# Two score components in separate PSUM tiles, a new engine order, and raw weight tiles with two buffers in a two-layer diffusion backbone

## The chip, the cores and the metric

The kernel runs on one core of a Trainium2 chip. The metric is the device time of one execution in microseconds; lower is better. The core has TensorE (PE; its weight loads are listed as PEld), VectorE (DVE), ScalarE (ACT), GpSimd (POOL) and SyncE (SP), each with its own queue of instructions that it takes in order. SP issues nearly all DMA transfers here, so a transfer whose data isn't ready holds up all that stand behind it in SP's queue.

## The reference, cut to what matters

Two layers over 1024 tokens of width 1024, with 256 context tokens. Layer 0 has a short gated convolution and differential attention with 4 heads side by side, layer 1 a Fourier mixing; a squared-ReLU MLP follows each. The change lies in layer 0, in the input projections and the attention:

```python
def diff_attend(q, k, v, lam):                     # c: two components of each head
    s = jnp.einsum('bqhcd,bkhcd->bhcqk', q, k).astype(jnp.float32) * (DIFF_QK_DIM ** -0.5)
    p = jax.nn.softmax(s, axis=-1)
    pd = (p[:, :, 0] - lam * p[:, :, 1]).astype(v.dtype)
    return jnp.einsum('bhqk,bkhd->bqhd', pd, v)

u = modulate(h, sh1, sc1)                          # sh, sc, g: silu(c) @ ada_w + ada_b
p = u @ w_in[j]                                    # conv (3 x 512), q, k, v columns
k_all = jnp.concatenate([k, kc], axis=1)           # 1024 latent + 256 context keys
o = diff_attention_blocks(q, k_all, v_all, lam)    # 128 queries at a time
y = jnp.concatenate([conv_mixer(...), sub_ln(o, ...)], axis=-1) @ w_out_mix[j]
```

## The kernel before, in words

All products are made of rounded parts: a tensor is split into a high part (`ScalarE` copy to fp32r) and a low part (the difference), and a product is three matmuls, lines 87 to 89 (`mm3`). Times in microseconds below are from the span's start.

**Projections.** Twenty weight tiles of 128x1024, eight for q and k and twelve for the convolution, are loaded by SP (`w_load`, line 218), split by ScalarE (line 97) and GpSimd (line 98) into `wh` and `wl` (`w_parts`), and used by TensorE (`proj`). The raw tile `wraw` has one buffer, `wh` and `wl` have two. `next_weights(i)` splits tile i+1 and then loads tile i+2. In the q/k part each of four passes (q and k, two pairs of heads) makes blocks of 512 tokens (b0, b1, and for k the 256 context tokens), which are rotated on VectorE, GpSimd and ScalarE (`rotate`) into the tiles `rp0` to `rp3`, two buffers each, and stored to DRAM (line 398). `store(0)` issues all waiting stores but the last entry, so each block's stores leave one block later.

Between them VectorE sums up the modulation vectors of the layer (`Ada`): one tick adds one 128x512 tile `wa` of `ada_w` (load line 152, addition lines 158 and 160); eight ticks make a unit, which `ada_end` finishes some ticks later with one matmul `ag` (line 174). Four units are gate rows: their bias row is loaded into a tile of the same ring (line 177), added (line 179), and one row is stored to DRAM at once (line 181). The ring has 6 tiles, and loads run 5 ahead. In this part the order of every queue, SP's too, is the order of the program. The second half of the units runs in the convolution part, with a new pool. After convolution tile 8 SP loads the q/k sets of the first head (`load_set`, lines 496 to 499, eight transfers each) and its values.

**Attention.** 32 query tiles (8 for each head) of 128 rows, two of them a pair. For component c of a tile: S makes the scores of 1280 keys (six matmuls, lines 615 to 619), M their negated maximum (VectorE, line 622), E the exponential and its sum (ScalarE, line 627). The one PSUM tile `scores`, 128 x 2 x 1280, holds both components for the whole stage; component 0 has columns 0 to 1279 with the context keys last, component 1 columns 1280 to 2559 with the context keys first. CB makes the factor lambda over the sums (VectorE), PD scales component 1 (GpSimd, line 636), PE adds it to component 0 (GpSimd, line 640, as two pieces because the keys are ordered differently). Then in five rounds for a pair: T transposes two key blocks of both tiles (TensorE, four operations, line 654, tile `pt`, two buffers), H rounds (ScalarE, line 660), L takes the rest (VectorE, line 665), P multiplies with the values (six matmuls into `po`). OC copies `po` out, SQ squares (GpSimd), SS sums over a head's width (TensorE), SC updates the norm (VectorE, two operations, lines 693 and 694).

The order of PE, DVE, ACT and POOL is written out by the table `PIPE`: the time of each step in pairs after the pair's start; all steps of all pairs are sorted by pair + offset and issued in that order. SP's order in this stage comes from a planner. FR, FS and FL finish the rows of a head (a product on GpSimd, a rounded copy on ScalarE, the rest on VectorE, each for four quarters of 256 columns), X times the split of the output weights. A q/k set is reloaded into the buffers of an older one (`load_set(n)`, three sets in turn). When the scores are done, their space becomes the accumulators `bky` of the output projection (`open_rows`), for which 28 groups of three matmuls (`prefill`) are spread over the remaining steps.

Of the kernel before, what the change touches and what calls it, by code (L numbers as in the profile page):

```python
# [12 lines left out]
F32 = mybir.dt.float32  # L13
F32R = mybir.dt.float32r
AF = mybir.ActivationFunctionType
ALU = mybir.AluOpType
# [4 lines left out]
P = 128  # L21
N = 1024
NC = 256
D = 1024
KT = 8
NK = N + NC
# [4 lines left out]
FS = 1.0 / math.sqrt(1024.0 * 128.0)  # L31
# [6 lines left out]
def body(tc, nc, I, O, dbg=None):  # L38
# [104 lines left out]
    modp = {}  # L143
    gates = {}

    def ada_unit(wp, psp, ptag, l, which, half, steps=False, wab=3, **kw):
        c0 = which * D + half * 512
        acc = []

        def load(k):  # L150
            wa = wp.tile([P, 512], F32, name="wa", tag="wa", bufs=wab)
            nc.sync.dma_start(out=wa, in_=I["ada_w"][l, k * P:(k + 1) * P, c0:c0 + 512])
            return wa

        def add(k, wa):
            if k == 0:
                acc.append(wp.tile([P, 512], F32, name="aacc", tag="aacc", bufs=2 if steps else 3))
                nc.vector.tensor_scalar(acc[0], wa, cs[:, k, 0:1], None, ALU.mult)
            else:
                nc.vector.scalar_tensor_tensor(out=acc[0], in0=wa, scalar=cs[:, k, 0:1], in1=acc[0],  # L160
                                               op0=ALU.mult, op1=ALU.add)

        finish = lambda: ada_end(wp, psp, ptag, l, which, half, acc[0], wab, **kw)
        if steps:
            return load, add, finish
        for k in range(KT):
            add(k, load(k))
        return finish

    def ada_end(wp, psp, ptag, l, which, half, acc, wab, gate=None, col=None, plus=False, spill=None):  # L170
        c0 = which * D + half * 512
        if True:
            ps = psp.tile([P, 512], F32, name="ag", tag=ptag)
            nc.tensor.matmul(ps, ones, acc, start=True, stop=True)
            if gate is not None or spill is not None:
                gb = wp.tile([P, 512], F32, name="wa", tag="wa", bufs=wab)
                nc.sync.dma_start(out=gb, in_=I["ada_b"][l, c0:c0 + 512].partition_broadcast(P))
                dst = gate[:, half * 512:half * 512 + 512] if spill is None else gb
                nc.vector.tensor_tensor(out=dst, in0=ps, in1=gb, op=ALU.add)
                if spill is not None:  # L180
                    nc.sync.dma_start(out=spill[:, half * 512:half * 512 + 512], in_=gb[0:1, :])
                return
            t = wp.tile([P, 4, P], F32, name="wa", tag="wa", bufs=wab)
            for j in range(4):
                nc.vector.tensor_tensor(out=t[:, j, :], in0=ps[:, j * P:(j + 1) * P], in1=ident, op=ALU.mult)
            d = col[:, half * 4:half * 4 + 4]
            nc.vector.tensor_reduce(out=d, in_=t, axis=AX.X, op=ALU.add)
            b = adab[:, l * 48 + which * 8 + half * 4:l * 48 + which * 8 + half * 4 + 4]
            nc.vector.tensor_tensor(out=d, in0=d, in1=b, op=ALU.add)
            if plus:  # L190
                nc.vector.tensor_scalar(d, d, 1.0, None, ALU.add)


    ps1 = popen("ps1", bufs=4, space=PSUM)
# [10 lines left out]
    gate = {}  # L205
# [8 lines left out]

    def w_load(i):
        if i < len(wsrc):
            wraws[i] = pW.tile([P, D], F32, name="wraw", tag="wraw", bufs=1)
            nc.sync.dma_start(out=wraws[i], in_=wsrc[i])

    def w_parts(i):  # L220
# [133 lines left out]
    ada0 += [(4, h, dict(col=col["sc2"], plus=True)) for h in range(2)]  # L354
    ada0 += [(3, h, dict(col=col["sh2"])) for h in range(2)]
    tile_waits = dict(reuse_waits="tile")


    class Ada:
        AHEAD = 5  # L360

        def __init__(self, p, units):
            self.units = [ada_unit(p, ps1, "tr", 0, w, h, steps=True, wab=self.AHEAD + 1, **kw) for w, h, kw in units]
            self.n, self.m, self.wa, self.ends = 0, 0, {}, []
            self.load(self.AHEAD)

# [23 lines left out]
    Qd = [dram.tile([4, 4, 32, N], F32, name=f"Qd{i}") for i in range(2)]  # L390
    Kd = [dram.tile([4, 4, 32, NK], F32, name=f"Kd{i}") for i in range(2)]
    Ad = [dram.tile([KT, P, N], F32, name=f"Ad{i}") for i in range(2)]
    stores = []

    def store(*keep):
        while len(stores) > len(keep):
            for o, i in stores.pop(0):
                nc.sync.dma_start(out=o, in_=i)

    def next_weights(i):  # L400
        if i:
            w_parts(i + 1)
        w_load(i + 2)

    def proj(i, bH, bL, n, tag="mm"):
        ps = ps1.tile([P, 512], F32, name="pj", tag=tag)
# [106 lines left out]
    with tc.manual_schedule(engines={mybir.EngineType.PE, mybir.EngineType.DVE, mybir.EngineType.Activation,  # L513
# [41 lines left out]
        for c in range(12):  # L555
            i = 8 + c
# [25 lines left out]
    pclose("pC", "pW", "pGs", "pU")  # L582
    psS = popen("psS", bufs=1, space=PSUM, **tile_waits)
    psT = popen("psT", bufs=1, space=PSUM, side="right", **tile_waits)
    scores = psS.tile([P, 2, NK], F32, name="s")
    pA = popen("pA", bufs=2, side="left", **tile_waits)
    pGate = popen("pGate", side="right", **tile_waits)
    for n in ("g1", "g2"):
# [11 lines left out]
    class Tile:  # L600
# [5 lines left out]
        def S(self, c):  # L606
            if not self.sc:
                self.mx = pA.tile([P, 2], F32, name="mx", tag="mx", bufs=4)
            H = hsets[self.h, c]
            q = H["q"][:, self.qt * P:self.qt * P + P]  # L610
            t = self.sc[c] = scores[:, c, :]
            x = NC * c
            for o in (0, 512):
                ps = t[:, x + o:x + o + 512]
                nc.tensor.matmul(ps, q, H["k0"][:, o:o + 512], start=True, stop=False)  # L615
                nc.tensor.matmul(ps, q, H["k1"][:, o:o + 512], start=False, stop=True)
            ps = t[:, 0:NC] if c else t[:, N:NK]
            nc.tensor.matmul(ps, q, H["k0"][:, N:NK], start=True, stop=False)
            nc.tensor.matmul(ps, q, H["kx"], start=False, stop=True)

# [15 lines left out]
            nc.gpsimd.tensor_scalar(self.e[1], self.e[1], self.a, 0.0, ALU.mult, ALU.add)  # L636

        def PE(self):
            for o, i in ((slice(0, N), slice(NC, NK)), (slice(N, NK), slice(0, NC))):
                nc.gpsimd.tensor_tensor(out=self.e[0][:, o], in0=self.e[0][:, o], in1=self.e[1][:, i], op=ALU.add)  # L640

    class Pair:
        def __init__(self, p):
# [3 lines left out]

        def T(self, kp):
            pd = [tiles[2 * self.p + j].e[0] for j in range(2)]
            pt = psT.tile([P, 2, 256], F32, name="pt", tag="pt", bufs=2)  # L650
            for i in range(2):
                for j in range(2):
                    kt = kp * 2 + i
                    nc.tensor.transpose(pt[:, i, j * P:(j + 1) * P], pd[j][:, kt * P:(kt + 1) * P], ident)
            self.pt[kp] = pt
# [71 lines left out]
    def finish_last(A7):  # L727
        H = heads[3]
        A7.extend(p3a.tile([P, N], F32R, name=f"A7{i}", tag=f"A7{i}", bufs=1) for i in range(2))
        for hf in range(2):  # L730
            bc = psT.tile([P, 512], F32, name="bc", tag="pt", bufs=2)
# [105 lines left out]
    for h in range(4):  # L837
        k = PIPE["SC",] + 4 * h + 3
        at(k + 0.001, lambda h=h: finish_stats(h))
        if h < 3:  # L840
            for m in range(4):
                base = k + 0.6 + (m if h < 2 else m // 2 * 0.8)
                fr = base + (PIPE["FR",] - base) % 1.0
                fs, fl = (fr + PIPE[o,] - PIPE["FR",] for o in ("FS", "FL"))
                for t, f in ((fr, finish_rows), (fs, finish_split), (fl, finish_low)):
# [600 lines left out]


PIPE = {
    ("FR",): -6.2830,
    ("FS",): -6.0349,  # L1450
    ("FL",): -5.9476,
    ("S", 1, 0): 0.0000,
    ("M", 1, 0): 0.1528,
    ("S", 0, 0): 0.2550,
    ("E", 1, 0): 0.3415,
    ("M", 0, 0): 0.4838,
    ("S", 1, 1): 0.5563,
    ("E", 0, 0): 0.6288,
    ("M", 1, 1): 0.6786,
    ("S", 0, 1): 0.7886,  # L1460
    ("CB", 0): 0.8122,
    ("E", 1, 1): 0.8236,
    ("PD", 0): 0.8690,
    ("M", 0, 1): 0.9188,
    ("PE", 0): 0.9878,
    ("E", 0, 1): 1.0638,
    ("CB", 1): 1.2865,
    ("PD", 1): 1.3432,
    ("PE", 1): 1.4620,
    ("T", 0): 1.9563,  # L1470
    ("H", 0): 2.0114,
    ("L", 0): 2.0917,
    ("T", 1): 2.1677,
    ("T", 2): 2.2114,
    ("H", 1): 2.2367,
    ("H", 2): 2.2891,
    ("L", 1): 2.3319,
    ("T", 3): 2.4044,
    ("L", 2): 2.4227,
    ("P", 0): 2.4480,  # L1480
    ("T", 4): 2.5127,
    ("H", 3): 2.5354,
    ("L", 3): 2.6175,
    ("P", 1): 2.6594,
    ("P", 2): 2.7240,
    ("H", 4): 2.7703,
    ("L", 4): 2.8576,
    ("P", 3): 2.8917,
    ("P", 4): 3.1031,
    ("OC",): 3.2052,  # L1490
    ("SQ",): 3.2585,
    ("SS",): 3.3581,
    ("SC",): 3.3930,
    ("X",): 4.4830,
}

PERM = np.concatenate([np.arange(512), [512], 1024 - np.arange(1, 512)])
# [109 lines left out]
```

## Time and profile before

| | us |
|---|---|
| median of 3 runs (lowest, highest) | 2466.03 (2465.24, 2471.18) |
| profiled execution, its own time | 2469.14 |
| its span, first to last instruction | 2467.3 |
| PE busy | 2232.9 (90%) |
| VectorE, GpSimd, ScalarE busy | 1263.8 (51%), 1031.7 (42%), 692.7 (28%) |
| mean granted clock of TensorE | 0.962 |
| projections; attention with TensorE's tail | 113 to 418; 418 to 757 |

A busy share is a mean over stages with different limits, so each stage has to be read for itself. A matmul's duration in a row is modelled, since matmuls overlap; the distance from one start to the next tells what one costs the engine. "[1.66 <-DVE mx L622]" says that the engine sat idle for 1.66 us before this instruction and that the maximum of line 622 on VectorE ended the wait. The granted clock is 1.0 at 2.4 GHz and 0.5 at 1.2 GHz.

### The profile page before, as it was taken

Reading aid. Unit: us, or ns where it says so; the run is one execution under the profiler, and the core shown is the slowest. Engines: PE = TensorE matmul, PEld = TensorE weight load, DVE = VectorE, ACT = ScalarE, POOL = GpSimd, SP = SyncE. Lnnn points to the kernel's source line nnn. Section 1 sums busy time; section 2 is a strip of 40 time slices with the busy share of each in tenths; the row PEclk is TensorE's granted clock in tenths of the full one; section 3 lists DMA queues with packets and bytes.
Section 4 is the critical chain, followed back from the end, with each engine's and each line's share of the span. In section 5 each row is a group of like instructions: output and inputs, shape, how many; then the busy total and the mean of one; then the engine's idle time right before and its main releaser. Section 6 shows DMA issues by size and latency. Waiting matters only on the chain.

```text
span 2467.3 us, 26198 instructions
## 1 busy us (share of the span) xinstructions
PE 2232.9 (90%) x9978; PEld 1795.7 (73%) x9978; DVE 1263.8 (51%) x1751; ACT 692.7 (28%) x1039; POOL 1031.7 (42%) x736
## 2 busy tenths in 40 slices
PE   7988597567779899999999999989899999999998
PEld 4776485456667687777788887767678888788886
DVE  7455362456654677567643433745653433434335
ACT  5211011345543521112112222443612212122122
POOL 3333131465653543323345834555733333334131
PEclk9998798799989999999999999999999999999999
DMA  7344438044323634334322323343511111111111
GB/s 280 128 155 140 155 128 212 31 98 119 83 69 111 209 112 155 105 113 141 101 68 82 127 92 107 113 156 120 180 51 52 52 35 60 43 52 52 45 50 68
DMA packets 121869, 261.98 MB, mean 106 GB/s; under 512 B 14642, under 2 KB 44594, under 8 KB 121488
## 3 DMA queue, kind: packets, MB, share of 16 engines
q1 hardware_dynamic: 120704, 254.69, 31.8%
q0 software_dynamic: 1040, 5.62, 0.7%
q8 instruction: 78, 1.28, 0.2%
q14 instruction: 47, 0.39, 0.0%
HBM read 213.06 MB, written 47.21 MB: 105 GB/s over the span
## 4 chain that ended last, share of the span: by engine, by line
PE 61%; DMA 11%; DVE 10%; POOL 7%; ACT 5%; issue 4%; SPq 1%; POOLq 0%; ACTq 0%; DVEq 0%
PE bky L87 9%; PE bky L88 9%; PE bky L89 9%; PE bkh L89 7%; PE bkh L88 7%; PE bkh L87 7%; DVE mx L622 3%; DMA wa<-in_ada_w 3%; ACT e L627 2%; DVE aacc L160 2%; DMA wa<-in_ada_b 2%; PE s L615 2%; DMA Kd<-rp 1%; PE pj L89 1%; PE pj L87 1%
## 5 line engine op out<-in xcount | busy, mean ns | idle before, releaser
L1016 DVE TENSOR_TENSOR acc<-bky,acc 128x512 f32<-128x512 f32 x448 | 304.3, 688 | 321.6 <-PE bky L89 320.5
L87 PE MATMUL bky<-wh,hh 128*128 128x512 f32 x1024 | 402.8, 395 | 16.8 <-DVE acc L1016 14.7
L88 PE MATMUL bky<-wl,hh 128*128 128x512 f32 x1024 | 402.4, 393 | 0.0
L89 PE MATMUL bky<-wh,hl 128*128 128x512 f32 x1024 | 401.3, 392 | 0.0
L1000 POOL TENSOR_TENSOR hl<-r,hh 128x512 fp32r<-128x512 f32 x128 | 178.9, 1401 | 407.2 <-DVE r L999 398.4
L963 ACT CAST wh<-wraw 128x1024 fp32r<-128x1024 f32 x128 | 131.4, 1049 | 674.2 <-PE bky L89 479.7
L964 POOL TENSOR_TENSOR wl<-wraw,wh 128x1024 fp32r<-128x1024 f32 x56 | 137.3, 2457 | 300.0 <-ACT wh L963 300.0
L999 DVE TENSOR_TENSOR r<-r 128x512 f32<-128x512 f32 x128 | 119.4, 939 | 243.8 <-ACT hh L998 240.1
L87 PEld LDWEIGHTS bky<-wh,hh 128*128 128x128 f32 x1024 | 192.7, 188 | 67.2 <-DVE acc L1016 21.2
L88 PEld LDWEIGHTS bky<-wl,hh 128*128 128x128 f32 x1024 | 192.8, 188 | 43.2 <-issue 0.7
L89 PEld LDWEIGHTS bky<-wh,hl 128*128 128x128 f32 x1024 | 192.8, 188 | 42.4
L88 PE MATMUL bkh<-UB,wh 128*128 128x512 f32 x512 | 200.9, 393 | 0.7 <-POOL UB L133 0.7
L87 PE MATMUL bkh<-UB,wh 128*128 128x512 f32 x512 | 200.7, 393 | 0.0
L89 PE MATMUL bkh<-UB,wl 128*128 128x512 f32 x512 | 200.6, 392 | 0.0
L962 POOL TENSOR_TENSOR wraw<-wraw,gateg 128x1024 f32<-128x1024 f32 x64 | 156.6, 2447 | 97.6 <-DMA wraw<-in_w 90.2
L87 PE MATMUL bkh<-UA,wh 128*128 128x512 f32 x448 | 177.9, 397 | 0.0
L88 PE MATMUL bkh<-UA,wh 128*128 128x512 f32 x448 | 176.3, 394 | 0.0
L89 PE MATMUL bkh<-UA,wl 128*128 128x512 f32 x448 | 175.7, 394 | 0.0
L87 PE MATMUL pj<-UH,wh 128*128 128x512 f32 x320 | 134.0, 419 | 41.2 <-ACT wh L97 41.2
L160 DVE SCALAR_TENSOR_TENSOR aacc<-wa,cs,aacc 128x512 f32<-128x512 f32 x140 | 141.9, 1014 | 37.3 <-DMA wa<-in_ada_w 34.9
L622 DVE TENSOR_REDUCE mx<-s 128x1 f32<-128x1280 f32 x64 | 95.5, 1492 | 125.5 <-ACT e L627 125.1
L964 DVE TENSOR_TENSOR wl<-wraw,wh 128x1024 fp32r<-128x1024 f32 x72 | 118.2, 1649 | 77.5 <-ACT wh L963 77.4
(386 smaller groups left out, 4250.8 us busy)
## 6 DMA issues: line engine op xcount, KB each, us to landing
wraw<-in_w SPq DMA_DIRECT2D x128, 512.0 KB
wa<-in_ada_w SPq DMA_DIRECT2D x160, 256.0 KB
xt<-in_ada_w SPq DMA_DIRECT2D x16, 512.0 KB
xt<-in_x SPq DMA_DIRECT2D x16, 512.0 KB
acc<-Hd SPq DMA_DIRECT2D x16, 512.0 KB
wraw<-in_w_cv SPq DMA_DIRECT2D x12, 512.0 KB
aa<-Ad SPq DMA_DIRECT2D x16, 384.0 KB
k<-Kd SPq DMA_DIRECT2D x16, 320.0 KB
```

Of the source, the lines that this page charges most:

```text
L87: nc.tensor.matmul(ps, aH, bH, start=start, stop=False)
L88: nc.tensor.matmul(ps, aH, bL, start=False, stop=False)
L89: nc.tensor.matmul(ps, aL, bH, start=False, stop=stop)
L160: nc.vector.scalar_tensor_tensor(out=acc[0], in0=wa, scalar=cs[:, k, 0:1], in1=acc[0], op0=ALU.mult, op1=ALU.add)
L615: nc.tensor.matmul(ps, q, H["k0"][:, o:o + 512], start=True, stop=False)
L622: nc.vector.tensor_reduce(out=self.mx[:, c:c + 1], in_=self.sc[c], axis=AX.X, op=ALU.max, negate=True)
L962: nc.gpsimd.tensor_tensor(out=w, in0=w, in1=g, op=ALU.mult)
L963: nc.scalar.copy(wh, w)
L964: eng.tensor_tensor(out=wl, in0=w, in1=raw(wh), op=ALU.subtract)
L999: nc.vector.tensor_tensor(out=r, in0=r, in1=r, op=ALU.mult)
L1000: pace[0] = nc.gpsimd.tensor_tensor(out=hl[:, c], in0=r, in1=raw(hh[:, c]), op=ALU.subtract)
L1016: pace[1] = nc.vector.tensor_tensor(out=a[:, c], in0=ps, in1=a[:, c], op=ALU.add)
```

## The change

Projections: `wraw` gets two buffers; `next_weights` loads tile i+2 before it splits tile i+1; the `Ada` ring has 8 tiles for loads 7 ahead, and the tiles of `ada_end` come from a ring of their own (`wf`, two); the store of a gate row is put on the list `stores` and issued with the next stores.

Attention: each component has its own PSUM tile of 1280 columns, with the context keys last in both, and a buffer of its own; GpSimd's addition is one operation of 1280 columns; `pt` has one buffer instead of two, also for the broadcast in `finish_last`; the times at which the quarters of a head's rows are finished follow one formula for heads 0 to 2 (line 842); and `PIPE` has new offsets, with a pair's last step at 2.99 instead of 3.39.

```diff
-    def ada_unit(wp, psp, ptag, l, which, half, steps=False, wab=3, **kw):
+    def ada_unit(wp, psp, ptag, l, which, half, steps=False, wab=3, stores=None, **kw):
...
-        finish = lambda: ada_end(wp, psp, ptag, l, which, half, acc[0], wab, **kw)
+        finish = lambda: ada_end(wp, psp, ptag, l, which, half, acc[0], *(("wf", 2) if steps else ("wa", wab)), stores, **kw)
...
-                gb = wp.tile([P, 512], F32, name="wa", tag="wa", bufs=wab)
+                gb = wp.tile([P, 512], F32, name="wa", tag=wtag, bufs=wab)
...
-                if spill is not None:
+                if stores is not None:
+                    stores.append([(spill[:, half * 512:half * 512 + 512], gb[0:1, :])])
+                elif spill is not None:
                     nc.sync.dma_start(out=spill[:, half * 512:half * 512 + 512], in_=gb[0:1, :])
...
-            wraws[i] = pW.tile([P, D], F32, name="wraw", tag="wraw", bufs=1)
+            wraws[i] = pW.tile([P, D], F32, name="wraw", tag="wraw")
...
-        AHEAD = 5
+        AHEAD = 7
...
     def next_weights(i):
+        w_load(i + 2)
         if i:
             w_parts(i + 1)
-        w_load(i + 2)
...
-    scores = psS.tile([P, 2, NK], F32, name="s")
...
-            t = self.sc[c] = scores[:, c, :]
-            x = NC * c
+            t = self.sc[c] = psS.tile([P, NK], F32, name=f"s{c}", tag=f"s{c}")
             for o in (0, 512):
-                ps = t[:, x + o:x + o + 512]
+                ps = t[:, o:o + 512]
...
-            ps = t[:, 0:NC] if c else t[:, N:NK]
+            ps = t[:, N:NK]
...
-            for o, i in ((slice(0, N), slice(NC, NK)), (slice(N, NK), slice(0, NC))):
-                nc.gpsimd.tensor_tensor(out=self.e[0][:, o], in0=self.e[0][:, o], in1=self.e[1][:, i], op=ALU.add)
+            nc.gpsimd.tensor_tensor(out=self.e[0], in0=self.e[0], in1=self.e[1], op=ALU.add)
...
-            pt = psT.tile([P, 2, 256], F32, name="pt", tag="pt", bufs=2)
+            pt = psT.tile([P, 2, 256], F32, name="pt", tag="pt", bufs=1)
...
-                base = k + 0.6 + (m if h < 2 else m // 2 * 0.8)
+                base = k + 0.6 + m // 2 * 0.8
```

The new order within one pair's time, by engine, where a prime marks a step of the next pair's rounds, is: PE: S(1) of tile 0, T2, P0, P1, T3, P2, S(0) of tile 0, T4, P3, S(1) of tile 1, T0', P4, S(0) of tile 1, T1', SS. DVE: FL, L2, CB1, M, L3, M, L4, M, L0', CB0, M, L1', SC. ACT: E, H2, FS, H3, X, E, H4, E, H0', E, OC, H1'. POOL: PE0, PD1, PE1, FR, X's low part, PD0, SQ.

## Rows read from the trace of the kernel before

**Rows 1.** Stretches: length; PE, PEld, DVE, ACT, POOL busy; clock, DMA, GB/s
```profile
113.00:418.00 305.00, 254.00 (x1074) 203.68 (x1073) 141.33 (x201) 39.02 (x54) 76.72 (x43) 0.90 0.50 157
308.00:398.00 90.00, 90.00 (x392) 73.16 (x390) 47.84 (x77) 13.59 (x18) 24.46 (x12) 1.00 0.57 160
...
457.00:720.00 263.00, 181.88 (x1092) 156.88 (x1092) 162.06 (x225) 133.42 (x218) 166.15 (x121) 0.93 0.33 81
720.00:757.00 37.00, 35.34 (x198) 31.04 (x198) 8.84 (x19) 7.99 (x16) 8.04 (x9) 0.91 0.31 89
```

**Rows 2.** Waits of SP's queue, 113 to 418: total us, times, longest
```profile
SPq L218 <- POOL wl L98: 52.3, 11, 9.4
SPq L181 <- DVE wa L179: 37.0, 4, 10.5
```

**Rows 3.** TensorE in time order, behind idle stretches: start, us, [idle <-releaser]
```profile
183.61 0.80 PE L87 MATMUL pj<-UH,wh 128*128 128x512 f32 x1 [8.03 <-ACT wh L97]
186.10 0.80 PE L89 MATMUL pj<-UH,wl 128*128 128x512 f32 x1 [1.27 <-POOL wl L98]
...
291.57 0.79 PE L87 MATMUL pj<-UH,wh 128*128 128x512 f32 x1 [17.44 <-ACT wh L97]
...
403.95 0.80 PE L87 MATMUL pj<-UH,wh 128*128 128x512 f32 x1 [5.75 <-ACT wh L97]
```

**Rows 4.** SP in order of time: bias row, gate-row store, weight loads
```profile
262.67 3.26 SPq L177 DMA_DIRECT2D wa<-in_ada_b  x1
276.53 0.26 SPq L181 DMA_DIRECT2D G2d<-wa  x1
...
282.16 0.40 SPq L218 DMA_DIRECT2D wraw<-in_w_cv  x1
...
394.71 0.36 SPq L218 DMA_DIRECT2D wraw<-in_w_cv  x1
```

**Rows 5.** Waits of the engines, 418 to 757: total us, times, longest
```profile
DVE mx L622 <- ACT e L627: 125.1, 62, 8.3
```

**Rows 6.** Attention in order of time, one turn of maximum, scores, exponential
```profile
584.58 1.49 DVE L622 TENSOR_REDUCE mx<-s 128x1 f32<-128x1280 f32 x1 [2.37 <-ACT e L627]
...
586.12 0.50 PE L615 MATMUL s<-k,q 128*128 128x512 f32 x1 [1.66 <-DVE mx L622]
...
587.39 0.28 PE L87 MATMUL po<-ph,vs 128*128 128x256 f32 x1
...
587.64 1.33 ACT L627 ACTIVATE e<-s,mx 128x1280 f32<-128x1280 f32 x1 [2.62 <-PE s L619]
...
588.09 0.60 PE L654 MATMUL pt<-ident,e 128*128 128x128 f32 x4
...
589.09 1.49 DVE L622 TENSOR_REDUCE mx<-s 128x1 f32<-128x1280 f32 x1 [2.05 <-ACT e L627]
```

**Rows 7.** Groups by shape, 418 to 757: count, busy us, mean ns, idle before
```profile
L640 POOL TENSOR_TENSOR e<-e,e 128x1024 f32<-128x1024 f32 x32 | 75.6, 2363 | 2.1
L665 DVE TENSOR_TENSOR pl<-pt,ph 128x512 fp32r<-128x512 f32 x80 | 54.5, 682 | 19.2 <-ACT ph L660 19.1
...
L660 ACT CAST ph<-pt 128x512 fp32r<-128x512 f32 x80 | 45.7, 586 | 21.7 <-PE po L89 15.5 <-PE pt L654 6.0
...
L640 POOL TENSOR_TENSOR e<-e,e 128x256 f32<-128x256 f32 x32 | 23.8, 743 | 0.0
```

**Rows 8.** Attention in order of time, the two steps of SC and GpSimd beside them
```profile
577.58 1.34 POOL L636 TENSOR_SCALAR e<-e,ca 128x1280 f32<-128x1280 f32 x1 [1.05 <-DVE ca L633]
...
577.99 0.93 DVE L693 SCALAR_TENSOR_TENSOR ss<-R 128x2 f32<-128x2 f32 x1
...
579.03 0.16 DVE L694 SCALAR_TENSOR_TENSOR ss<-po,ss 128x2 f32<-128x2 f32 x1
```

**Rows 9.** TensorE in order of time, first scores of component 0 of head 1
```profile
504.12 0.50 PE L615 MATMUL s<-k,q 128*128 128x512 f32 x1 [1.46 <-DMA wor<-in_w_out]
```

**Rows 10.** ScalarE in order of time, start of attention
```profile
431.46 1.06 ACT L1076 ACTIVATE gateg<-gateg 128x1024 f32<-128x1024 f32 x1 [7.41 <-DMA gateg<-in_ln_g]
```

More of the change, by code (lines that the diff above doesn't have):

```diff
@@ L168, in ada_unit, with ada_end @@
         return finish
-    def ada_end(wp, psp, ptag, l, which, half, acc, wab, gate=None, col=None, plus=False, spill=None):
+    def ada_end(wp, psp, ptag, l, which, half, acc, wtag, wab, stores, gate=None, col=None, plus=False, spill=None):
         c0 = which * D + half * 512
@@ L179, in ada_end @@
                 nc.vector.tensor_tensor(out=dst, in0=ps, in1=gb, op=ALU.add)
-                if spill is not None:
+                if stores is not None:
+                    stores.append([(spill[:, half * 512:half * 512 + 512], gb[0:1, :])])
+                elif spill is not None:
                     nc.sync.dma_start(out=spill[:, half * 512:half * 512 + 512], in_=gb[0:1, :])
                 return
-            t = wp.tile([P, 4, P], F32, name="wa", tag="wa", bufs=wab)
+            t = wp.tile([P, 4, P], F32, name="wa", tag=wtag, bufs=wab)
             for j in range(4):
@@ L356, in body, with store @@
     tile_waits = dict(reuse_waits="tile")
+    stores = []
+    def store(*keep):
+        while len(stores) > len(keep):
+            for o, i in stores.pop(0):
+                nc.sync.dma_start(out=o, in_=i)
     class Ada:
-        AHEAD = 5
+        AHEAD = 7
         def __init__(self, p, units):
-            self.units = [ada_unit(p, ps1, "tr", 0, w, h, steps=True, wab=self.AHEAD + 1, **kw) for w, h, kw in units]
+            self.units = [ada_unit(p, ps1, "tr", 0, w, h, steps=True, wab=self.AHEAD + 1, stores=stores, **kw) for w, h, kw in units]
             self.n, self.m, self.wa, self.ends = 0, 0, {}, []
@@ L392, in body @@
     Ad = [dram.tile([KT, P, N], F32, name=f"Ad{i}") for i in range(2)]
[L393 to L398, printed above, removed]
     def next_weights(i):
+        w_load(i + 2)
         if i:
             w_parts(i + 1)
-        w_load(i + 2)
     def proj(i, bH, bL, n, tag="mm"):
@@ L730, in finish_last @@
         for hf in range(2):
-            bc = psT.tile([P, 512], F32, name="bc", tag="pt", bufs=2)
+            bc = psT.tile([P, 512], F32, name="bc", tag="pt", bufs=1)
             for j in range(4):
@@ L1448 @@
 PIPE = {
-    ("FR",): -6.2830,
-    ("FS",): -6.0349,
-    ("FL",): -5.9476,
+    ("X",): -9.6372,
+    ("FR",): -9.5434,
+    ("FS",): -8.8084,
+    ("FL",): -7.9375,
     ("S", 1, 0): 0.0000,
[L1453 to L1494, printed above, removed]
+    ("M", 1, 0): 0.3034,
+    ("S", 0, 0): 0.3526,
+    ("E", 1, 0): 0.4332,
+    ("M", 0, 0): 0.4777,
+    ("S", 1, 1): 0.5700,
+    ("E", 0, 0): 0.6075,
+    ("M", 1, 1): 0.6724,
+    ("S", 0, 1): 0.7592,
+    ("CB", 0): 0.7920,
+    ("E", 1, 1): 0.8163,
+    ("PD", 0): 0.8428,
+    ("M", 0, 1): 0.8874,
+    ("E", 0, 1): 1.0180,
+    ("PE", 0): 1.0297,
+    ("CB", 1): 1.1548,
+    ("PD", 1): 1.2721,
+    ("PE", 1): 1.3784,
+    ("T", 0): 1.6732,
+    ("H", 0): 1.7224,
+    ("L", 0): 1.7858,
+    ("T", 1): 1.8624,
+    ("H", 1): 1.9242,
+    ("L", 1): 1.9812,
+    ("T", 2): 2.0461,
+    ("P", 0): 2.0852,
+    ("H", 2): 2.0977,
+    ("P", 1): 2.1431,
+    ("L", 2): 2.1548,
+    ("T", 3): 2.2197,
+    ("H", 3): 2.2690,
+    ("L", 3): 2.3292,
+    ("P", 2): 2.3511,
+    ("T", 4): 2.4089,
+    ("H", 4): 2.4660,
+    ("L", 4): 2.5231,
+    ("P", 3): 2.5684,
+    ("P", 4): 2.7576,
+    ("OC",): 2.8491,
+    ("SQ",): 2.8874,
+    ("SS",): 2.9515,
+    ("SC",): 2.9891,
 }
```

## The prediction

> **What bounds the kernel now.** I read the busy time of the engines by stage first, then in each stage who waited for whom, then single instructions in order of time. From 790 us on TensorE is the bound and the change touches nothing there, so two stages matter.
>
> The first is the projections, 113 to 418 us. TensorE is busy for 254.0 of 305 us [rows 1], so it idles for 51 us. Where nothing disturbs it, 392 matmuls take 90.0 us at full clock, 0.23 us each [rows 1]. The 1074 matmuls of the stage, 96 of them of half width by the code, would need 978 x 0.23 + 96 x 0.115 = 236 us; the other 18 us of the busy time are matmuls at the lower granted clock (mean 0.90), mostly just behind an idle stretch. There are six such stretches: 183.6, 201.3, 237.5, 258.8, 291.6 and 404.0; the shortest waits for a modulation sum, the other five for the rounded copy of the next weight tile (`wh`), three of which stand in [rows 3]. Behind them is SP's queue: for 52 us it stood at a weight load because GpSimd had not yet finished with the only raw tile, and for 37 us at the four gate-row stores, each of which waits for a bias row that was issued just before it [rows 2]. The stretch that ends at 291.6 shows it whole: bias row issued at 262.7, its store at 276.5, and only then the weight load, at 282.2 [rows 4]. The stretches at 183.6 and 258.8 are the same delay at second hand: Q and K stores came late, so ScalarE's rotary copies, queued ahead of the weight copy, waited for their buffers.
>
> The second is attention, 418 to 720 us for 16 pairs, and TensorE's tail to 757. Here no engine is the bound: in the long stretch PE is busy 69%, GpSimd 63%, VectorE 62% [rows 1]. VectorE's maximum waits for ScalarE's exponential 62 times in 64 [rows 5], though it reads other columns. In order of time, maximum, scores and exponential never overlap: maximum at 584.58, scores at 586.12, exponential at 587.64, next maximum at 589.09 [rows 6]. That is 4.51 us for each component, 18.05 us for a pair of query tiles. The two components meet at column 1280, inside the 512-column block 1024 to 1535 that both use.
>
> The Trainium skill (PSUM — Partial Sum Buffer, PSUM bank collisions raise a hardware error) says that two engines must not touch one 2 KiB bank in the same partitions together, two readers included, so that they have to be ordered by bank and not by address. By that rule the wait goes with the shared block. If it came from the small tile `mx` that both components share instead, it would stay inside a tile, and cost about 0.5 us of a pair, 8 us in all; the 62 waits include those of the next tile, which has another `mx`, so the trace sides with the rule.
>
> **The change part by part.** *Scores apart.* Component 1 no longer waits for component 0, and the 18.05 us are gone. What is late next? Per pair (263 / 18.05 = 14.6 pairs) the engines need PE 12.5, GpSimd 11.4, VectorE 11.1, ScalarE 9.2 us [rows 1]; that is the lower bound, 12.5. But the queues are in order and hand over to each other. I followed the new order once round from the end of the third low part (L2): CB 0.4 (two operations like the 0.16 of [rows 8]), M 1.5, L 0.7, T 0.6, P 0.7, S until its maximum can start 1.5, M 1.5, L 0.7, CB 0.4, PD 1.35, SQ 0.75 (as a GpSimd operation of 256 columns), SS 0.4 (estimate), S as TensorE's queue sees it 1.3, T 0.6, H 0.6, L 0.7: 13.7 us [rows 6 to 8]. I take 13.7 and keep 12.5 to 15.8 (below).
>
> To this come, over the stage: two bursts in which the rows of a head are finished, all four quarters at once, 4 us of VectorE; the same bursts beside the low parts of the output weights on GpSimd, whose sum is nearly full, 6; TensorE at half clock now and then, as in 0.93 of [rows 1], 4; ScalarE's wait of 7.4 us for the gain of the first layer norm, at the start of the stage [rows 10], of which I leave 4 on the path. And the reload of a q/k set: it may start when the old set's last scores are out and must land before component 0 of the next head. Before, that distance was 0.70 x 18.05 = 12.6 us, and still the scores waited 1.46 [rows 9]; after, it is 0.78 x 13.7 = 10.7. So 2.7 us at three heads, 8. Sum 26. The loop: 15 x 13.7 + 14 for the last pair + 26 = 245.5 against 302: **57 us less** (12.5 gives 76, 15.8 gives 24).
>
> *One transpose bank.* T waits for the L before it: 0.6 + 0.6 + 0.7 with hand-overs 2.0 us, five times 10 us of 13.7. It fits; without the slack it would cost what each H or L stands behind E or M (a rival below). The broadcast of the last head's norms uses the same tag and is put in series: under 1 us.
>
> *One addition instead of two* on GpSimd: 2.36 + 0.74 becomes some 2.95 by their slope, 0.15 us in each of 32 tiles, inside the 13.7.
>
> *Tail.* Behind the last exponential TensorE is busy for 35.3 of 37 us [rows 1]; 28 output matmul groups that need the scores' space (28 x 3 x 0.23 = 19 us) stay there. The new order is less far behind by about one P stage: 3 us less (0 to 10).
>
> *Weight tiles doubled, load ahead of the split.* The load's buffer is then free long before, so SP's 52 us go. *Gate rows stored late:* SP no longer stands at the bias row's landing. Longer modulation ring with two tiles for the ends: SP stays at most about two sums ahead of VectorE either way, so nothing by itself. Stretch by stretch, with the wait for `wl` behind it (8.03 + 1.27 [rows 3], from 51 in all): 183.6: 9.3 to 0.5; 201.3: 3.6 to 0; 237.5: 3.3 to 0.7; 258.8: 8.9 to 1. At 291.6 the last gate row is stored by the final drain, with the new ring's seven loads and the weight load queued behind it on SP, and TensorE waiting for that weight: it still pays the bias row's 10 to 13 us of landing, so 18.9 goes to 9 only. At 404.0 the weight load stands behind two whole q/k sets on SP and is issued at 394.7 [rows 4]; this is the same after: 7 stays. Saved 33 us, and 5 of the 18 us at half clock (at 183.6, 201.3, 258.8): **38 us** (20 to 50: the low end if Q and K stores still land late).
>
> *Sum:* 57 + 3 + 38 = 98. The profiled execution took 2469.1 us, 3.1 above the median of the runs: 2469.1 - 98 - 3.1 = **2368 us**.
>
> **The rivals.** *The engines' sum alone decides* (12.5 us a pair): 19 us less, 2349. For it: all busy shares are then about 0.9; against it: queues are in order and each step crosses engines.
>
> *The shared port:* the first step of SC, 128x2, ran 0.93 us, to the end of GpSimd's PD that began before it [rows 8]; its sibling with an input from PSUM took 0.16. In the new order it stands beside the 2.95 us addition. I count this as hidden, since L2 comes 2.9 us later anyway. If half of it shows, 1.4 us in 16 pairs: 2390.
> The Trainium skill (SBUF — State Buffer, Who interferes with whom) has it that a VectorE operation with two SBUF inputs and a GpSimd operation that reads SBUF exclude each other for the whole instruction. The 0.93 agrees; by the rule this rival takes all 2.9 us where L2 isn't late itself.
>
> *The change doesn't part the components:* if the second tile began inside the first one's last block, the 4.51 us chain would stay, and only projections gain: 2466 - 38 = 2428. For it only that 1280 is no multiple of 512.
>
> *Slower: one transpose bank.* If every H stands behind an E (1.4) and every L behind an M (1.5), a round takes 4.9 us and a pair 24.5: 16 x 6.45 = 103 us more, less 38: 2531. It decides from a pair of 18.05 + 41/16 = 20.6 us, a round of 4.1. Against it: by the order only L3, L4 and L0 stand right behind an M, and these maxima run while T and H do. If two of five rounds suffer, a pair takes 17 and the time is 2421.
>
> **How the numbers follow.** Forecast 0.61; engines' sum 0.12; port 0.10; not parted 0.05; transpose bank in part 0.06, in full 0.03; anything else slower 0.01; level 0.02. The range: period 12.5 to 15.8 is -19 to +33, projections -12 to +18, tail -7 to +3, not all at once: 2330 to 2412. It holds forecast, engines' sum and port; it leaves out the last cases, and some of the tails of the first, under 0.2. Within 0.3% (7 us, about what a measurement of this kernel can tell from no change) is 0.02, slower 0.04, faster 0.94.
>
> **What would show it.** After the change the maximum should wait for TensorE or for nothing, not for the exponential, and maxima come 13.7 us a pair apart over four. The wait of SP's weight loads for GpSimd is gone; stretches before `wh` remain at two places only. Wrong it would be if the pair takes 16 us or more, if the waits of `pt` for `pl` carry the loop, or if the projections still lose over 30 us to idle.

## The result and the profile after

| | before | after |
|---|---|---|
| median of the runs made together, us | 2468.6 | 2394.4 (2389.4 to 2396.3) |
| ratio, 95% interval | | 0.9694 (0.9667 to 0.9720) |
| span of the profiled execution, us | 2467.3 | 2394.5 |

Forecast was 2368 us in a range of 2330 to 2412: the sign and the range held, the size did not. 98 us were to go and 74 went. The two spans, cut at the same marks, show where (us; in the first column the mark that ends each part):

| part, up to | before | after | change | forecast |
|---|---|---|---|---|
| last matmul of the values | 113.6 | 107.0 | -6.6 | 0 |
| projections, to the first matmul of the scores | 304.7 | 293.9 | -10.8 | -38 |
| attention, to the end of the last exponential | 302.6 | 238.4 | -64.2 | -57 |
| TensorE's tail, to the last norm | 35.6 | 32.7 | -2.9 | -3 |
| all that follows | 1710.8 | 1722.5 | +11.7 | 0 |

The last row is mostly the scatter of single executions: the twelve other kernels below, with nearly the same work there, have 1714 to 1721 us, so in these two executions before was quick and after slow in that part. Not all of it need be scatter: the five executions with one tile or the old order have 1711 to 1717 us there, the nine with two tiles and the new order 1717 to 1723, 4.4 us more in the mean. The cause of that is open. The loss against the forecast lies mainly in the projections.

Stretches of after (length; PE, PEld, DVE, ACT, POOL busy; clock, DMA share, GB/s), to be read beside [rows 1]:

```profile
106.00:400.00 294.00, 249.75 (x1074) 200.92 (x1073) 141.88 (x201) 38.83 (x54) 76.54 (x43) 0.92 0.52 163
...
440.00:620.00 180.00, 147.70 (x910) 131.60 (x910) 125.75 (x181) 108.92 (x177) 134.96 (x77) 0.91 0.46 110
640.00:672.00 32.00, 31.75 (x184) 27.45 (x182) 9.38 (x19) 7.96 (x15) 6.90 (x5) 0.96 0.36 105
```

In the attention loop PE went from 69% busy to 82%, GpSimd from 63% to 75%. In the projections TensorE still idles for 44 us, where before had 51.

Who waited in the loop of after, 400 to 640 us (total us, times, longest):

```profile
PE po L684 <- POOL sq L680: 30.3, 14, 3.9
...
ACT e L626 <- DVE mx L621: 17.3, 38, 2.9
DVE mx L621 <- PE s L618: 14.6, 34, 1.6
...
PE pt L652 <- DVE pl L663: 1.5, 2, 1.3
```

The 62 waits of the maximum for the exponential [rows 5] are gone; it waits for TensorE, 14.6 us in all. At the single transposing buffer TensorE waits 1.5 us. Its longest wait in the loop, 30.3 us in 14 pieces, is at SS for the squares (SQ) of GpSimd, a step of the chain that the forecast followed. One turn in order of time, against [rows 6], where maximum, scores and exponential stood nose to tail:

```profile
505.37 1.34 ACT L626 ACTIVATE e<-s,mx 128x1280 f32<-128x1280 f32 x1
505.74 1.49 DVE L621 TENSOR_REDUCE mx<-s 128x1 f32<-128x1280 f32 x1 [0.24 <-PE s L618]
506.85 0.50 PE L614 MATMUL s<-k,q 128*128 128x512 f32 x1
507.27 1.33 ACT L626 ACTIVATE e<-s,mx 128x1280 f32<-128x1280 f32 x1
508.34 1.49 DVE L621 TENSOR_REDUCE mx<-s 128x1 f32<-128x1280 f32 x1 [0.34 <-PE s L618]
```

At 505.74 the maximum of one component runs beside the exponential of the other, and the next scores begin while it is still running. The period is in the summary of the tile `s` (duration min, median, max in ns, first and last start):

```profile
L621 DVE TENSOR_REDUCE mx<-s x64: 1478/1491/1493, 402.2 to 636.4; 128x1 f32<-128x1280 f32 x64
```

63 steps in 234.2 us are 14.9 us for a pair. Taken one by one, five of the fifteen distances from pair to pair are 11.4 to 13.8 us, and the two longest are 19.3 and 19.5.

The projections of after: what VectorE and SP waited for, then TensorE behind its longest idle stretches, as in [rows 2] and [rows 3]:

```profile
DVE wa L179 <- DMA wa<-in_ada_b: 44.4, 4, 12.3
...
SPq L152 <- DVE aacc L160: 64.7, 22, 11.7
SPq L220 <- POOL wl L98: 14.3, 3, 6.3
```

```profile
178.19 0.79 PE L87 MATMUL pj<-UH,wh 128*128 128x512 f32 x1 [9.25 <-ACT wh L97]
...
274.80 0.80 PE L87 MATMUL pj<-UH,wh 128*128 128x512 f32 x1 [16.01 <-ACT wh L97]
...
385.45 0.79 PE L87 MATMUL pj<-UH,wh 128*128 128x512 f32 x1 [5.37 <-ACT wh L97]
```

SP's wait for GpSimd fell from 52.3 to 14.3 us, and its 37.0 us at the gate-row stores are gone. But VectorE still stands 44 us at the four bias rows, 10 to 12 us each, and SP waits longer at the ring: 64.7 us for VectorE's sums, where before had 22.9. (That wait is not by itself a loss: a kernel below has 59.4 us of it and one idle stretch left.) Of the six stretches five remain within 2 us; only the one that before had at 258.8 fell clearly, from 8.9 to 1.7 us.

### The profile page after: what moved, and what is told of

The parts are those of the page before. It is cut to its first block, busy times and chain, and to the rows that moved or that the text cites. A ratio compares the mean times of both kernels' runs of the same rounds, so it can differ in the third digit from the quotient of the medians.

```text
span 2394.5 us, 26145 instructions
## 1 busy us (share of the span) xinstructions
PE 2220.9 (93%) x9978; PEld 1791.4 (75%) x9978; DVE 1255.8 (52%) x1751; ACT 695.3 (29%) x1039; POOL 1025.7 (43%) x704
## 3 DMA queue, kind: packets, MB, share of 16 engines
q8 instruction: 78, 1.28, 0.2%
## 4 chain that ended last, share of the span: by engine, by line
PE 61%; DMA 12%; POOL 8%; DVE 8%; issue 5%; ACT 2%; SPq 2%; POOLq 0%; DVEq 0%; ACTq 0%
PE bky L87 10%; PE bky L88 10%; PE bky L89 9%; PE bkh L89 8%; PE bkh L88 8%; PE bkh L87 8%; DMA wa<-in_ada_w 3%; DVE aacc L160 2%; DMA wa<-in_ada_b 1%; DMA Kd<-rp 1%; DMA k<-Kd 1%; PE pj L89 1%; PE pj L87 1%; PE pj L88 1%; POOL ra L889 1%
## 5 line engine op out<-in xcount | busy, mean ns | idle before, releaser
L995 ACT ACTIVATE r<-bkh 128x512 f32<-128x512 f32 x120 | 70.7, 595 | 294.8 <-PE bkh L89 283.5
```

The source lines that it names most:

```text
L995: nc.scalar.activation(r, ps, AF.Relu)
```

## The experiments

Each run is timed against runs of before on the same chip; times are medians and the ratio is to before.

**The two halves alone.** First the attention half of the diff on the kernel before, then the projection half.

> The attention half of the change alone, projections as before. If the two halves add up and the 12 us that the changed kernel loses behind attention belong to this half, 2468.6 - 64 - 3 + 12 = 2413 us. If those 12 us are chance or belong to the other half, 2401 us. The first scores start at 418 us, as before, and the last exponential ends 238 us later (before: 302).

> The projection half alone, attention as before. If the bias rows of the gates still hold VectorE, and through the ring of modulation tiles SP, the first scores start near 401 us as in the changed kernel and the time is 2468.6 - 17 = 2451 us. If my forecast of this half was right and something of the other half spoiled it, they start near 380 us and the time is 2430 us.

Measured: attention alone 2400.2 us, ratio 0.9719 (0.9691 to 0.9748); projections alone 2463.9, ratio 0.9977 (0.9961 to 0.9994). The halves add up within the intervals: 70 and 6 us against 74 together. For the attention half the second case came, 2401 without the 12 us. For the projection half neither time did: the first scores came where the first case had them, but the time is 13 us above its 2451. So the projection half was worth a sixth of the 38 us that were forecast, and some of it is given back: alone it brought the first scores from 418.3 to 399.4 us, but the first exponential, which waits for the gain of the layer norm, only from 422.6 to 413.8.

**The second raw tile alone**, on the kernel before.

```diff
-            wraws[i] = pW.tile([P, D], F32, name="wraw", tag="wraw", bufs=1)
+            wraws[i] = pW.tile([P, D], F32, name="wraw", tag="wraw")
...
+        w_load(i + 2)
         if i:
             w_parts(i + 1)
-        w_load(i + 2)
```

> The kernel before with one edit: two buffers for the raw weight tile, and each weight load issued ahead of the split of the next. Gate rows and ring as before. Theory (the second buffer is what the projection half gains, above all 6.6 us in the values' stage, where ScalarE no longer stands 11.9 us at its cast of a weight; the gates' late rows gain nothing, because VectorE still stands at the bias row): 2460 to 2465 us, no slower than the whole projection half alone (2463.9). Rival (the late gate rows and the deeper ring give what there is): within 2 us of before, 2467 us.

Measured: 2468.8 us, ratio 0.9987 (0.9969 to 1.0004). The interval holds no change as well as a gain of 7 us, so the time decides for neither expectation. The profiled execution says more: its first scores start at 403.5 us, 14.8 earlier than before, where the whole half has 18.9 (399.4). So most of what the half gains up to there is the second raw tile. In this run SP still stands at the gate-row stores for 35.9 us; the late gate rows and the longer ring, which end that, add 4.1 us. The values end at 106.7 us, 6.9 earlier, as in after. That term I had not seen: with one raw tile ScalarE stood in the values' stage at the cast of the second weight tile, ahead of the copies of the values.

```profile
95.78 1.05 ACT L97 CAST wh<-wraw 128x1024 fp32r<-128x1024 f32 x1 [11.90 <-DMA wraw<-in_w_qk]
```

This is ScalarE in the kernel before; in after no such wait is left there.

**Tiles and order, one without the other.** The kernel after with the old `PIPE` and the old spread of the finishing steps; then the kernel after with its new order, but with one tile for both components, the addition in two pieces and two transposing banks.

> The kernel after with the engine order of before (each key of the order as it was, and the finishing bursts spread as before); scores in tiles of their own, one transposing bank and the whole projection half stay. Theory (the tiles apart carry the loop's gain: they end the waits of the maximum for the other component's exponential, 62 waits and 125 us in before): most of the loop's 64 us stays, S to the last exponential at most 260 us where after has 238.4, 2395 to 2418 us. Rival (the new order carries it: without it the turn M, S, E stays nose to tail on VectorE and TensorE stands behind the single transposing bank): the loop stays at 280 us or more, 2435 us or more.

> The kernel after with the scores of both components back in one tile (the second shifted so that they share a bank), the addition back in two parts and two transposing banks, but in the new engine order and with the projection half. The other corner to the run with the tiles apart in the old order (2452.3 us, loop 299 us from S to the last exponential). Theory now (neither half works alone: the tiles apart leave only six banks and so one transposing bank, which the old order's back-to-back transposes stand 72 us at; and the order alone leaves the maximum behind the other component's exponential): the waits of the maximum for the exponential stay above 60 us, S to the last exponential 270 to 300 us, 2430 to 2455 us. Rival (the order alone carries the gain): S to the last exponential under 255 us, 2410 us or less.

Measured, with the stage from the first scores to the last exponential:

| scores | order | stage, us | median, us | ratio |
|---|---|---|---|---|
| one tile | old (before) | 302.6 | 2468.6 | 1 |
| two tiles | old | 299.0 | 2452.3 | 0.9926 (0.9901 to 0.9952) |
| one tile | new | 341.3 | 2494.8 | 1.0100 (1.0080 to 1.0121) |
| two tiles | new (after) | 238.4 | 2394.4 | 0.9694 (0.9667 to 0.9720) |

The three lower rows have the projection half too. Both single-cause theories fell: two tiles alone gain 4 us in this stage, and the order alone costs 39 us. The last is more than either text of the second run expected (270 to 300 us, or under 255). The waits say where. Two tiles in the old order, 420 to 740 us:

```profile
PE pt L652 <- DVE pl L663: 71.8, 51, 2.5
...
DVE mx L621 <- PE s L618: 55.4, 26, 3.3
```

One tile in the new order, 400 to 740 us:

```profile
ACT e L628 <- PE s L620: 166.9, 61, 4.7
...
DVE mx L623 <- ACT e L628: 134.8, 48, 12.7
```

With two tiles the maximum no longer waits for the exponential, though the components still share `mx`; so the common block was the cause and not that small tile. But with two tiles the transposes have one buffer, and the old order issues them nose to tail: TensorE stands 72 us there. The new order spreads the transposes (1.5 us in after), but with one tile the maximum still waits for the exponential.

**The shared port.** In after VectorE's first step of SC once waits out the whole of GpSimd's addition, as the rival said, and TensorE stands behind it, since `po` has one buffer:

```profile
558.24 2.92 POOL L638 TENSOR_TENSOR e<-e,e 128x1280 f32<-128x1280 f32 x1
558.33 2.84 DVE L691 SCALAR_TENSOR_TENSOR ss<-R 128x2 f32<-128x2 f32 x1
561.28 0.16 DVE L692 SCALAR_TENSOR_TENSOR ss<-po,ss 128x2 f32<-128x2 f32 x1
...
561.49 0.39 PE L87 MATMUL po<-ph,vs 128*128 128x256 f32 x1 [0.85 <-DVE ss L692]
```

The next run computes that first step behind CB, while GpSimd waits for `ca`:

```diff
+            r0 = r[:, 0:1]
+            d = heads[self.h]["ss"][:, self.qt:self.qt + 1]
+            nc.vector.tensor_scalar(d, r0, r0, SUB_EPS, ALU.mult, ALU.mult)
...
-            r0 = heads[self.h]["R"][:, q, 0]
-            nc.vector.scalar_tensor_tensor(out=d, in0=r0, scalar=SUB_EPS, in1=r0, op0=ALU.mult, op1=ALU.mult)
```

> The changed kernel, with the first step of SC (the square of the sums times epsilon, which in the trace stood beside GpSimd's addition for up to 2.8 us) issued right behind CB for each tile, when GpSimd waits for CB. If that wait lies on the path of the pair, 0.8 to 1.5 us go in each of 16 pairs: 2370 to 2382 us. If the pair is set elsewhere, since the next L isn't ready sooner anyway, the time stays within 3 us of 2394.

Measured: 2391.0 us, ratio 0.9676 (0.9651 to 0.9701), which overlaps the interval of after; the stage took 242.5 us against 238.4. The wait is real, but no gain from moving it can be told from none. It is also rarer than I had it: in 13 of its 16 places the step took 0.15 to 0.4 us, in the others 2.84, 1.28 and 0.92, so that all there was to gain is 4.6 us. The edit is not free either: 32 steps of 0.2 us stand in place of the 16.

**The bias row early.** The kernel after, with the bias row of each gate loaded with the last weight tile of its unit, in place of after the unit's matmul.

```diff
+            if steps and k == KT - 1 and "spill" in kw:
+                rows.append(wp.tile([P, 512], F32, name="wa", tag="wf", bufs=2))
+                nc.sync.dma_start(out=rows[0], in_=I["ada_b"][l, c0:c0 + 512].partition_broadcast(P))
```

> The changed kernel, with each gate's bias row loaded together with the last weight tile of its unit, some eleven ticks before it is added. If VectorE's four waits for that row (44 us) are what keeps SP at the ring and so the weight loads and stores late, these waits go, the idle stretches before the weight copies at 180, 198 and 232 us shrink to under 2 us each and that at 277 us to about 8, and the projections are 20 to 28 us shorter: 2370 us. If transfers are simply too slow or the rotary buffers hold ScalarE by themselves, the stretches stay and the time is 2390 to 2396 us.

Measured: 2380.7 us, ratio 0.9637 (0.9614 to 0.9660), 14 us less than after; first scores at 389.6 us. VectorE's waits for the bias rows are gone and the first scores come 11.3 us earlier, so the cause is right, at half its price (20 to 28): before two weight tiles TensorE still idles 7.1 us (to 177.0) and 14.7 us (to 264.8).

**What holds the rest: buffers, SP's order, or the transfers.** On top of the early bias row: three buffers for the rotated parts (`rp3`); then also the load of weight tile 10 ahead of the drain of stores, that of tile 19 ahead of the q/k sets, and the scaling of the gain moved into the loop (`best`); then, in place of these two moves, three raw tiles and every weight load one block earlier (`wraw3`).

> The kernel after with each gate's bias row loaded with the last weight tile of its unit (2380.7 us) and, on top, three buffers in place of two for the rotated parts. Theory (what is left at 169 to 177 and 190 to 195 us is VectorE and ScalarE standing 11 us at parts whose stores leave one block late): those waits on the stores go, the two stretches shrink by 8 to 12 us together, 2368 to 2374 us. Rival (the ring of weight tiles is fed late anyway, so another wait takes over): within 3 us of 2380.7.

> The previous one with three moves more: the weight load for the third convolution block (its index 10) issued before SP takes up the last stores and the spilled rows, the last weight load issued ahead of the two sets of q and k, and the multiplication of the first gain's row by alpha moved from ahead of the loop to behind its second pair. Theory (SP's place in line is what holds the weights: the stretches of 16 and 8 us that are left before weight casts, and 7.4 us in which ScalarE stands at the gain's row ahead of the first exponential): first scores at 360 to 370 us where the bias row's version has 389.6, 2340 to 2355 us. Rival (DMA engines, not SP's place, hold the weights): 2362 us or more.

> The run called best (bias row early, three buffers for rotated parts, gain's row scaled inside the loop; 2364.9 us) with three raw weight buffers and every weight load issued one block of projections earlier, in place of its two single moves. Theory (a weight load still stands in SP's line behind the Kd stores, whose four issues take 9.1 us at 168.96, and behind the ring: 12.1 us of TensorE at 179.7 and 11.4 at 282): those stretches fall to 2 us or less, first scores at 350 to 358 us where best has 373.6, 2342 to 2352 us. Rival (the DMA engines, not SP's line, are full there): first scores at 366 us or later, 2358 us or more.

Measured: 2383.9 us (0.9651, 0.9616 to 0.9685), 2364.9 (0.9576, 0.9541 to 0.9610) and 2361.8 (0.9556, 0.9539 to 0.9574); first scores at 388.1, 373.6 and 377.1. By their times none of the three theories held. `rp3` gained nothing that can be told from noise, and `wraw3` hardly anything on `best`. But `best` took 19 us off `rp3`, 14 of them ahead of the first scores, about half of what was asked: SP's place in line is part of it. What the rivals gave as the reason, DMA engines that are full, is wrong too, as the rows below show. With three buffers the waits for the stores of K went, and an idle stretch of 12 us came at 180 us, before the next weight tile. With every load a block earlier TensorE idled 14.2 us before 268.6, now for a modulation sum of VectorE, whose ring loads stood behind the stores. So neither buffers nor SP's order were the whole. SP's own row in `wraw3` points to the rest (start, time that the issue took), and before had it too:

```profile
222.46 28.56 SPq L368 DMA_DIRECT2D Kd<-rp  x12
```

```profile
240.78 21.84 SPq L398 DMA_DIRECT2D Kd<-rp  x8
```

In the first, twelve stores take SP 28.6 us to issue, 2.4 us each, where the issue of a weight load mostly takes 0.3 to 0.5. I read it as SP standing until the transfers ahead make room. And in that time the DMA engines are hardly used. From `wraw3`, and under it the same from before and from after:

```profile
240.00:250.00 10.00, 10.00 (x46) 8.29 (x45) 0.00 (x0) 0.00 (x0) 0.00 (x0) 1.00 0.26 102
```

```profile
240.00:260.00 20.00, 12.36 (x47) 9.25 (x46) 5.58 (x8) 5.14 (x9) 5.07 (x7) 0.84 0.26 94
```

```profile
240.00:250.00 10.00, 8.27 (x36) 6.45 (x35) 2.65 (x4) 3.82 (x7) 3.71 (x5) 1.00 0.26 102
```

A DMA share of 0.26 at 94 to 102 GB/s is a quarter of the 16 engines. A store's target here was `dst[:, i, :, c]`, 4 groups of 32 rows: its slowest dimension is 4. The Trainium skill (DMA: Bandwidth & Descriptors, Rules for kernel authors) says that the slowest dimension sets how many engines carry a transfer, so that one of size 4 is confined to four at most. The 0.26 agrees, and the next two runs test it.

**The stores as 128 rows.** The same tensors in DRAM, laid out as 4 x 128 rows, so that a store's slowest dimension is its 128 rows; a load of a q/k set becomes two of 32 rows each. On after, then on `wraw3`.

```diff
-    Qd = [dram.tile([4, 4, 32, N], F32, name=f"Qd{i}") for i in range(2)]
+    Qd = [dram.tile([4, P, N], F32, name=f"Qd{i}") for i in range(2)]
...
-        return [(dst[:, i, :, c], raw(parts[i])) for i in range(4)]
+        return [(dst[i, :, c], raw(parts[i])) for i in range(4)]
```

> The kernel after with one edit: the stored q and k lie as 4 x 128 rows in DRAM in place of 4 x 4 x 32, so that each store's slowest dimension is its 128 rows and not 4 groups; each of the loads of a set of q and k becomes two of 32 rows. In after, while only these stores are under way (240 to 250 us), the DMA share stands at 0.26 and 102 GB/s, a quarter of the 16 engines. Theory (this is the common cause of what is left in the projections: bias rows, ring and weights stand behind stores that four engines carry): the DMA share in that stretch doubles at least, the 18.7 us stretch before 277 us falls under 6 us, and the two at 169 to 198 us halve; first scores at 372 to 382 us where after has 400.9, 2367 to 2376 us. Rival (the writes themselves are slow, or the time lies in SP's order): first scores at 395 us or later, 2388 us or more.

> The same edit on top of the run wraw3 (bias row early, three buffers for rotated parts and raw weights, gain's row scaled inside the loop; 2361.8 us, first scores at 377.1). Theory (the stores on four engines hold the weights): the stretches of 11.0, 16.5 and 34.3 us that it still has at 198, 228 and 267 us go nearly whole, first scores at 330 to 342 us, 2318 to 2332 us. Rival (SP's order or VectorE holds them): 2355 us or more.

(The three stretches that the last text gives for `wraw3` are misread: its idle stretches are 1.8 us before 198, 6.4 before 231 and 14.2 before 268.6. The misread three sum to 61.8 us, more than the 35 to 47 us that were expected at the first scores. In the same way the 11.4 us that the text of `wraw3` gives for `best` at 282 are 1.9.)

Measured: on after 2347.0 us, ratio 0.9487 (0.9463 to 0.9510), 47 us less than after by this one edit; on `wraw3` 2332.8, ratio 0.9430 (0.9405 to 0.9455), the best kernel here. The first scores start at 354.4 and 342.7 us. On after that is more than the theory asked, on `wraw3` it misses the late edge of both its ranges by under 1 us (342 us, 2332 us). The stretches of the projections, on after and on `wraw3`:

```profile
107.00:354.00 247.00, 239.44 (x1072) 196.30 (x1071) 143.26 (x201) 38.83 (x54) 76.75 (x43) 0.98 0.62 194
```

```profile
107.00:342.00 235.00, 235.00 (x1069) 193.73 (x1068) 141.62 (x201) 38.27 (x54) 76.75 (x43) 1.00 0.64 202
```

In the second one TensorE is busy for 235.0 of 235 us at full clock: nothing is left to gain in this stage but work. On after, the one stretch that stays, 7.6 us, is the weight load behind the q/k sets. And the bias rows, whose code is that of after, cost VectorE little more than a quarter, while SP's wait at the ring is nearly what it was in after (waits as above, 107 to 356 us for VectorE, 106 to 380 for SP):

```profile
DVE wa L179 <- DMA wa<-in_ada_b: 12.4, 3, 4.2
...
SPq L152 <- DVE aacc L160: 59.4, 23, 11.7
```

So the 10 to 12 us of a bias row were for the most part not its own: they came from the stores ahead of it.

## Why the prediction was partly right

*The bound, right.* Both stages were the right ones, and the block that the two components share was the cause of the waits of [rows 5]: parted, they are gone, in the old order too.

*The loop, right in mechanism, a little short.* 64 us against 57, well inside 24 to 76. The sum was 15 x 13.7 + 14 + 26 = 245.5, measured 238.4. The period with all disturbances in it is 14.9, and 15 x 14.9 + 14 is 237.5: if an undisturbed pair takes the 13.7 of the forecast, as the quietest pairs do, the disturbances cost 18, not 26. Their pieces and the chain behind the 13.7 were not tested one by one. That the order and the tiles need each other stood in the text only in part: the rival "not parted" took the old loop's time for granted, 2428 us, where the new order with one tile made 2494.8, though a loop with one tile loses more in the new order than in the old.

*The transposing bank, right for this order.* Five rounds fitted; the waits are 1.5 us. In the old order the same bank costs 72 us, the danger that this rival described. (Its 17 us a pair do not follow from its rounds: two of 4.9 and three of 2.0 us are 15.8.)

*The port, right that it is mostly hidden.* Moved away, it changes nothing beyond the measurement. The rival's time of 2390 us lies nearer to the 2394.4 than the forecast does, but by chance: its cause can be 4.6 us at most.

*The tail, right:* 2.9 us against 3.

*The projections, wrong: the step that failed is "SP no longer stands at the bias row's landing", taken to end the idle stretches.* The term of 38 us measured 10.8 in its stage. Of its two parts the 5 us at half clock came at 4, but the 33 us of idle came at 7. By stretch, named by its place in before, with the wait for `wl` behind it:

| stretch | before | forecast | after |
|---|---|---|---|
| 183.6 | 9.3 | 0.5 | 10.5 |
| 201.3 | 3.6 | 0 | 4.3 |
| 237.5 | 3.3 | 0.7 | 3.4 |
| 258.8 | 8.9 | 1 | 1.7 |
| 291.6 | 18.9 | 9 | 17.4 |
| 404.0 | 7 | 7 | 6.6 |

The statement on SP was true, its 37.0 us did go, but with the ring's change that was worth 4.1 us at the first scores. SP was not the only queue at that landing: VectorE adds the bias row before it goes on. VectorE's wait was in the trace of before, and I had left it out:

```profile
DVE wa L179 <- DMA wa<-in_ada_b: 43.6, 4, 12.3
```

With this wait gone as well (the bias row early), the first scores came another 11.3 us earlier. My own condition for being wrong, more than 30 us of idle in the projections, is met with 44, and stretches before `wh` remain at four places and not two.

*The root was a level deeper.* I took 10 to 13 us as the price of a bias row, and "the low end if Q and K stores still land late" as a mishap. The row of before at 240 to 260 us shows a DMA share of 0.26 beside a TensorE that idles for 7.6 of 20 us, and that is a question: what is slow if not the engines? SP's row of before at 240.78, 21.8 us for eight issues, stood beside it. With it asked, the change that pays most in this stage, 47 us, is not in the diff at all: it brought the first scores 46.5 us forward with the bias rows loaded as late as in after.

*Left out:* the 6.6 us in the values' stage, the second raw tile's work. It is the same edit at a place that I had not looked at, since the first use of the tile lies ahead of the stage.

*Chances.* "Over 30 us of idle" had no rival of its own; it was only the low end of a term. A case "VectorE stays at the bias row", 33 us less gained, would have given 2401. The total also hides part of the misses: 27 us too little from the projections and 12 us behind attention stand against 7 more from the loop and 7 from the values, for which there was no term. That these two came is luck.

## What to carry to other kernels

When a wait is taken off one queue, look for every other queue that waits for the same landing; here SP's turn gave 4 us and VectorE's 11. When a transfer lands late while the DMA share is low, as here at 0.26, look at what stands ahead of it in the queue, and at the slowest dimension of those transfers. A long wait is not yet a cost: SP's wait at the ring stayed when the time fell. A bank freed and an order that uses it can be worth nothing apart and everything together, so test them as a square of four.

## What the runs showed of the hardware that I had not expected

Stores whose target is 4 x 32 rows moved 94 to 102 GB/s at a DMA share of 0.26, while SP took 2.4 us (`wraw3`) or 2.7 us (before) to issue each of them. As 128 rows, on after, twelve stores of K in the same place took SP 10 us to issue (19.9 in after) and no longer hold up the weights, and the stretch in which loads follow them shows 353 GB/s:

```profile
202.91 7.97 SPq L364 DMA_DIRECT2D Kd<-rp  x8
...
211.47 2.02 SPq L364 DMA_DIRECT2D Kd<-rp  x4
```

```profile
220.00:230.00 10.00, 10.00 (x46) 8.29 (x45) 5.49 (x8) 1.64 (x2) 2.28 (x1) 1.00 1.01 353
```

So a transfer's issue can be what blocks SP without standing in the list of waits: the 28.6 us of `wraw3` have no releaser, they are only in the length of the issue. That it is a full queue behind four engines was not seen directly. What is shown is that the new layout takes the time away. It also moves the rows in DRAM and splits the loads of the q/k sets, and how many engines carried a store stands in no trace.
